# A hybrid decoder block on one core: gate corners in Y, another order in the b0 units, the second step's weights by quarters

## The chip, the core and the metric

The kernel runs on one core of a Trainium2 chip. The metric is the device time of one execution in microseconds, the median of several runs. A core has TensorE (PE) for matmuls, VectorE (DVE), ScalarE (ACT), GpSimd (POOL) and SyncE (SP). Each works through its own instructions in order. Here SP issues the weight loads, and POOL issues the transfers of gates, operands and rows.

## The reference, cut to what matters

```python
h = rmsnorm(x, norm_w)                                   # 256 tokens x 4096
u_p, z_p, u_c, b_c, c_c, z_c, g = split(h @ w_in)        # 6 x 2048 and 2 x 4096 columns
y_pool = pool(u_p, pool_w, pool_scale) * silu(z_p)
y_conv = b_c * conv3(c_c * u_c) * silu(z_c)
br0, br1 = y_pool @ w_branch[0], y_conv @ w_branch[1]    # 2048 -> 4096 each
merged = sigmoid(g0 + gate_b0) * br0 + sigmoid(g1 + gate_b1) * br1
out = rmsnorm(x + merged @ w_out, final_norm_w)
```

All is float32, and the weights (474 MB) are read once.

## The kernel before

**Units and steps.** The work is a list of units, each giving 1024 output columns for the 256 tokens: four conv units for each of two halves (cz, cb, cu, cc), pool units (pz, pu), eight gate units g0_0, g1_0, g0_1, ... g1_3, eight branch units b0_0, b1_0, b0_1, ... b1_3, and four output units o0 to o3. A unit has 16 steps (8 in a branch unit), each of which takes 256 input channels and 1 MB of weights. To keep precision, every operand is split into a rounded part and a remainder, and each product is three matmuls. A P step is the plain product of 2 x 2 blocks, 24 matmuls. An S step replaces the 8 block products by 7 (a Strassen-like scheme with sums of blocks), 21 matmuls. A string for each unit gives the order, such as `EIGHT = "PSPSPSPSPSPSPSPS"`; `B0 = "PPPPPSPS"` is that of the four b0 units and `B1 = "PSPSPSPP"` that of the b1 units.

**Weights.** A load on SP brings a step's weights into one of three raw buffers (`NRAW`, `issue_load`, L884). ACT rounds them into cells of a ring of 15 (`highs`, L205), DVE writes the remainders (`lows`, L209). For an S step DVE first adds up four sums into the tile `parts`, and ACT and DVE split these too. A load is issued when the step three places earlier in the list `loaded` has been prepared. Preparation runs some steps ahead of PE (`pump`, L899), as far as ring cells are free; the order in which instructions are written there is the order in which each engine runs them.

**Ends of units.** PE accumulates in four banks `sums` (E in the code) and, for S steps, four banks `shared` (F). When a bank of `sums` closes, ACT evacuates it to the tile E. The `shared` banks are copied by ACT to a place for four corners, `join.slot`, and DVE makes three sums there (`corner_sums`, L379). `combine` (L389) adds them to E. For most units the slot is a raw buffer: a Join stands in the list of loads and takes its turn (L868). For branch units (`rotates = False`) it is the tile `last_pair`, called `spare()`. If the last step is an S step, its matmuls are reordered so that `sums` closes first (`closing`, L346).

**Epilogues.** After a unit a queue of small jobs runs, one for each tick, that is for every six matmuls; `gap(n)` is n empty ticks. A gate unit (L617) has two accumulating transfers add the bias to E (`gather`, POOL), later two sigmoids on ACT and a store. A b0 unit multiplies its gate, loaded to Y, by E one tick after its end (`gap(1)`, L635). A b1 unit multiplies by the second gate, adds Y and transposes on PE. In the last gate unit and the branch units the operands of later units are filled in as well: POOL loads to stages sa and sb, ACT and DVE split them into `arena` (`pop_fill`, L726).

**The opening.** The first unit's operands are made from x as its steps go: `fetch_x(j)` loads step j's piece to Y, ACT scales and rounds it, DVE makes the remainder. In the code x's first piece is issued first (L961), then step 1's weights in four quarters, so that each can be rounded as it lands; step 2's piece and weights follow, these in one load. For step 3 and some later ones DVE also makes sums of operand blocks, with a copy in the tile `extra`.

Of the kernel before, what the change touches and what calls it, by code (L numbers as in the profile page):

```python
# [17 lines left out]
D = 4096  # L18
HALF = D // 2
NU = 1024  # L20
# [18 lines left out]
EIGHT = "PSPSPSPSPSPSPSPS"  # L39
HOST = "PPPBPPMMPPSPSSPSSPS"  # L40
OUT3 = "PSPSPSPSPSPSSPPP"
B0 = "PPPPPSPS"
B1 = "PSPSPSPP"


# [1 line left out]
def hybrid_block(ctx: ExitStack, tc: tile.TileContext, x, xc, prm, rows_in, w_in, pool_w, w_branch, w_out, out):  # L47
# [5 lines left out]
    def act(dst, src, func=AF.Copy, **kw):  # L53
        return pin(nc.scalar.activation(dst, src, func, **kw))  # L54

    def tt(dst, a, b, op):
        return pin(nc.vector.tensor_tensor(out=dst, in0=a, in1=b, op=op))  # L57

    def mul(dst, a, b):
        return tt(dst, a, b, ALU.mult)  # L60

    def add(dst, a, b):
        return tt(dst, a, b, ALU.add)
# [7 lines left out]
    def load(dst, src):  # L71
        return pin(nc.sync.dma_start(dst, src))
# [4 lines left out]
    def gather(dst, src):  # L77
        return pin(nc.gpsimd.dma_start(dst, src, accum_op=ALU.add))  # L78
# [6 lines left out]
    def sb(name, shape, dt=F32):  # L85
        return const.tile(shape, dt, name=name)
# [4 lines left out]
    E = sb("E", [P, 2, NU])  # L91
    Y = sb("Y", [P, 2, NU])
# [42 lines left out]
    last_pair = {}  # L135
# [69 lines left out]
    def highs(cells, src):  # L205
        for i, c in runs(cells):
            act(ring[:, c, 0], src[:, i])

    def lows(cells, src):  # L209
        for i, c in runs(cells):  # L210
            sub(ring[:, c, 1], src[:, i], ring[:, c, 0].bitcast(F32))
# [7 lines left out]
    def quarters(tile_):  # L219
        return tile_.rearrange("p a (b c) -> p (a b) c", c=NH)  # L220

    class Step:
# [7 lines left out]
        def first(self):  # L230
            if self.kind == "B":
                return []

            def rounded(cells):
                self.q = self.raw.rearrange("p (i c) -> p i c", i=4)
                self.cells = cells
                if self is steps[0]:
                    for i in range(4):
                        highs(cells[i:i + 1], self.q[:, i:i + 1])
                else:  # L240
                    highs(cells, self.q[:, 0:len(cells)])

            return [(3 if self.kind == "S" else 4, None, rounded)]

        def rest(self):
            if self.kind == "P":
                def rests(_):
                    if self is steps[0]:
                        for i in range(4):
                            lows(self.cells[i:i + 1], self.q[:, i:i + 1])  # L250
                    else:
                        lows(self.cells, self.q)

                return [(None, None, rests)] + self.mid
            if self.kind == "S":
                def added(_):
                    q = self.q
                    add(sums[:, 0:2], q[:, 3:4].to_broadcast([P, 2, NH]), q[:, 1:3])
                    add(sums[:, 2], sums[:, 0], q[:, 2])
                    add(sums[:, 3], sums[:, 2], q[:, 0])  # L260
                    lows(self.cells, q[:, 0:3])

                def split(cells):
                    self.sum_cells = cells
                    highs(cells[0:2], sums[:, 0:2])
                    highs(cells[2:4], sums[:, 2:4])
                    lows(cells, sums)

                return [(None, None, added)] + self.mid + [(4, None, split)]
            if self.kind == "B":  # L270
                def parts(cells):
                    self.cells = cells
                    highs(cells, quarters(E))
                    lows(cells, quarters(E))

                return [(4, lambda: self.unit.flags.get("base"), parts)]

            def pooled(cells):
                self.pool_cells = cells
                q = quarters(E)[:, 2 * self.g:2 * self.g + 2]  # L280
                highs(cells, q)
                lows(cells, q)

            return [(None, None, lambda _: lows(self.cells, self.q)),
                    (2, lambda: self.unit.flags.get(f"pooled{self.g}"), pooled)]
# [155 lines left out]
    def gap(n):  # L441
        return [None] * n
# [23 lines left out]
    def seq_x(text):  # L466
        if text is FIRST:
            return [("P", i) for i in FIRST]
        return sequence(text, ND, ND + NS + NB, NB)
# [4 lines left out]
    def in_unit(name, col, epi, text, **kw):  # L474
        units.append(Unit(name, lambda i: w_in[col // NU, i], seq_x(text), x_ops, epi, scaled=True, **kw))
        units[-1].text = text
        return units[-1]
# [139 lines left out]
    def gate_unit(n, c):  # L617
        def epi(u):
            def bias(t):
                gather(E[:, t], gate_b[n, None, c * NU:(c + 1) * NU].to_broadcast([P, NU]))  # L620

            return gap(1) + [lambda: bias(0), lambda: bias(1)] + gap(12) + [
                lambda: act(E[:, 0], E[:, 0], AF.Sigmoid), None,
                lambda: act(E[:, 1], E[:, 1], AF.Sigmoid), lambda: move(gates_d[n, c], E)] + (
                    [lambda: move(Y, gates_d[0, 0])] if (n, c) == (1, 3) else [])
        text = HOST if (n, c) == (0, 0) else SIX4 if (n, c) == (1, 3) else EIGHT
        in_unit(f"g{n}_{c}", 6 * HALF + n * D + c * NU, epi, text)

    def spare():
        return last_pair["tile"].rearrange("p (a n) -> p a n", a=2)  # L630

    def branch_unit(n, c):
        def epi(u):
            if n == 0:
                return gap(1) + [lambda: mul(Y, E, Y)]  # L635
            turned = spare() if c < 3 else Y

            def gated():
                mul(E, E, spare())
                if c == 3:  # L640
                    last_pair["stack"].close()
                    open_last(F32R)
                    last_pair["again"] = True

            def copy(j):
                act(chan(turned)[:, 2 * j:2 * j + 2], bankview(j))

            def stored():
                put(m_d[c], chan(turned))
                merged[c] = now[0] + STORED  # L650
            return [lambda: move(spare(), gates_d[1, c])] + gap(6) + [gated, lambda: add(E, E, Y), None,
                lambda: c < 3 and move(Y, gates_d[0, c + 1])] + gap(3) + pairs(transposes(E, copy)) + [stored]

        text = B1 if n else B0
        u = Unit(f"b{n}_{c}", lambda i: w_branch[n, c, i], seq_y(text), y_ops[n], epi)
        u.urgent, u.lead, u.rotates = (lambda: None), 3, False
        units.append(u)
# [106 lines left out]
    steps = [s for u in units for s in u.steps]  # L764
# [43 lines left out]
    def fetch_x(j):  # L808
        load(xt[:, j % 4].rearrange("p o c -> p (o c)"), xc[first_order[j]])
# [74 lines left out]
    def issue_load(s):  # L884
        i = s.load_index
        r = raw[:, i % NRAW]
        if isinstance(s, Join):
            s.slot = r.rearrange("p (i c) -> p i c", i=4)
            return
        if i == 0:  # L890
            for k in range(4):
                load(r[:, k * NH:(k + 1) * NH], s.src[:, k * NH:(k + 1) * NH])
        else:
            load(r, s.src)
        if i + 1 < 16:
            fetch_x(i + 1)
        s.raw = r
# [60 lines left out]
            state["limit"] = state["now"] + u.lead  # L958
        pump()

    fetch_x(0)  # L961
    pump()

    def room(o):
# [36 lines left out]
    for u in units:  # L1001
        if u.name == "b0_0":
            last_pair["stack"].close()
            open_last(F32)
        if not u.rotates:
            u.join.slot = last_pair["tile"].rearrange("p (i c) -> p i c", i=4)
        if u is last_x:
            bands_open.close()
            more = ctx.enter_context(tc.tile_pool(name="more", bufs=1))
            stages.append(more.tile([P, 8, P], F32, name="sb"))  # L1010
            queue_fills()
        if u is last:
            break
        for st in u.steps:
            assert st.prepared, (u.name, st.kind)
            run_step(u, st)
            state["now"] += 1
            if state["now"] == OPENED:
                opening.close()
                sums = ctx.enter_context(tc.tile_pool(name="parts", bufs=1)).tile([P, 4, NH], F32, name="parts")  # L1020
            pump()
            if u.before and st is u.steps[len(u.steps) * 3 // 4]:
                flush()
                u.before()
        flush()
        combine(u)
        queue.extend(u.epi(u))
        pump()
# [102 lines left out]
```

## Time and profile before

| | us |
|---|---|
| median of three runs | 2419.91 (2418.51 to 2421.69) |
| the profiled execution | 2420.03 |
| its span, first to last instruction | 2418.3 |
| PE busy | 2379.8 |
| DVE busy | 2137.6 |
| ACT busy | 1421.8 |

The span is divided as follows. The first unit's matmuls begin at 5.95 us, g1_3 ends and b0_0 begins at about 1708 to 1716 us, and the last matmul ends at 2406.9. PE's busy time is no measure of speed by itself, since matmuls overlap, but its idle time is time in which no matmul ran. In rows of the timeline the numbers are start and length in us; square brackets give the engine's idle time before the row and what ended it. L57 and L54 are helpers that record nearly all DVE and ACT work, so the tile names tell the operations apart.

### The profile page before, as it was taken

The page shows a single profiled execution, that of the slowest core. Times are in us where ns is not written, and L with a number is a line of the kernel's source. Part 1 is how long each engine was busy: PE and PEld are TensorE (multiplying, and loading weights), DVE is VectorE, ACT ScalarE, POOL GpSimd, SP SyncE. Part 2 cuts the span into 40 slices and gives each one's busy share as a digit, 9 for nine tenths or more (in the row PEclk, how much of TensorE's full clock was granted, in tenths as well). Part 3 has the DMA queues.
Part 4 walks back from the last instruction along what each step waited for, and adds up shares of the span by engine and source line. Part 5 has one row for each costly group of instructions (what it writes and reads, how often), then busy time and mean ns, then how long its engine had stood idle before and what let it go on. Part 6 is the DMA issues. An engine that isn't in the chain of part 4 may idle for free. (4 is left out here: it accounts for less than half of the span.)

```text
span 2418.3 us, 26848 instructions
## 1 busy us (share of the span) xinstructions
PE 2379.8 (98%) x10515; PEld 1960.6 (81%) x10515; DVE 2137.6 (88%) x1769; ACT 1421.8 (59%) x1367; POOL 85.6 (4%) x147
## 2 busy tenths in 40 slices
PE   8999999999999999999999999999899999999998
PEld 6888888888888888888888888888778887888886
DVE  8789989988989969969998999889788889899998
ACT  6655555655556556556666566665565555556664
POOL 0000000000000000000000000001100000000000
PEclk9999999999999999999999999999999999999999
DMA  8656546655646655655776576667666765758767
GB/s 331 225 193 226 191 175 244 234 199 204 220 177 231 228 192 192 225 191 187 266 244 204 215 261 242 209 224 272 229 245 212 264 233 208 257 192 273 246 217 267
DMA packets 82959, 547.07 MB, mean 226 GB/s; under 512 B 9488, under 2 KB 9488, under 8 KB 21776
## 3 DMA queue, kind: packets, MB, share of 16 engines
q1 hardware_dynamic: 69392, 485.52, 55.1%
q0 software_dynamic: 13008, 58.73, 8.0%
q8 instruction: 82, 1.34, 0.2%
q10 hardware_dynamic: 432, 1.11, 0.1%
q14 instruction: 45, 0.37, 0.0%
HBM read 519.10 MB, written 26.21 MB: 225 GB/s over the span
## 5 line engine op out<-in xcount | busy, mean ns | idle before, releaser
L937 PE MATMUL sums<-ring,arena 128*128 128x512 f32 x7515 | 1756.9, 391 | 20.5 <-DVE ring L57 9.4
L937 PEld LDWEIGHTS sums<-ring,arena 128*128 128x128 f32 x7515 | 1412.2, 188 | 319.7 <-DVE ring L57 12.3
L57 DVE TENSOR_TENSOR ring<-raw,ring 128x2048 fp32r<-128x2048 f32 (+3 forms) x526 | 938.6, 1796 | 167.0 <-ACT ring L54 163.5
L54 ACT ACTIVATE ring<-raw 128x2048 fp32r<-128x2048 f32 (+3 forms) x526 | 791.4, 1520 | 493.9 <-PE sums L937 270.9
L54 ACT ACTIVATE ring<-parts 128x1024 fp32r<-128x1024 f32 (+1 forms) x403 | 400.2, 1007 | 384.2 <-DVE parts L57 341.6
L937 PE MATMUL shared<-ring,arena 128*128 128x512 f32 x2100 | 509.2, 391 | 1.5 <-DVE ring L57 1.5
L57 DVE TENSOR_TENSOR ring<-parts,ring 128x2048 fp32r<-128x2048 f32 (+3 forms) x225 | 434.9, 1946 | 44.5 <-ACT ring L54 43.6
L937 PEld LDWEIGHTS shared<-ring,arena 128*128 128x128 f32 x2100 | 396.3, 189 | 86.3 <-DVE ring L57 3.6
L57 DVE TENSOR_TENSOR parts<-parts,raw 128x512 f32<-128x512 f32 x378 | 262.0, 693 | 12.9
L57 DVE TENSOR_TENSOR parts<-raw 128x1024 f32<-128x1024 f32 x189 | 230.8, 1221 | 7.5 <-DMA raw<-in_w_in_dram 7.2
L937 PE MATMUL sums<-ring,last_pair 128*128 128x512 f32 x366 | 89.8, 396 | 0.0
L937 PEld LDWEIGHTS sums<-ring,last_pair 128*128 128x128 f32 x366 | 68.9, 188 | 16.5
L57 DVE TENSOR_TENSOR raw<-raw 128x512 f32<-128x512 f32 (+1 forms) x66 | 57.3, 868 | 10.9 <-ACT raw L54 9.3
L54 ACT ACTIVATE E<-sums,rin 128x512 f32<-128x512 f32 x56 | 36.0, 687 | 25.5 <-PE sums L937 25.4
L54 ACT ACTIVATE raw<-shared 128x512 f32<-128x512 f32 x88 | 47.0, 606 | 0.3
L937 PE MATMUL shared<-ring,last_pair 128*128 128x512 f32 x168 | 41.6, 396 | 0.0
L937 PEld LDWEIGHTS shared<-ring,last_pair 128*128 128x128 f32 x168 | 31.6, 188 | 7.7
L69 DVE SCALAR_TENSOR_TENSOR E<-raw,rin,E 128x1024 f32<-128x1024 f32 x28 | 34.7, 1280 | 0.2
L54 ACT ACTIVATE last_pair<-shared 128x512 f32<-128x512 f32 x44 | 24.2, 600 | 13.8 <-PE shared L422 13.1
L57 DVE TENSOR_TENSOR E<-E,last_pair 128x2048 f32<-128x2048 f32 x12 | 27.4, 2287 | 2.2 <-ACT E L54 2.2
L78 POOL DMA_DIRECT2D E<-in_rows_dram x16 | 13.9, 867 | 434.4 <-DVE E L69 432.3
L54 ACT ACTIVATE E<-sums 128x512 f32<-128x512 f32 x44 | 25.6, 596 | 2.9 <-PE sums L937 0.5
(118 smaller groups left out, 553.9 us busy)
## 6 DMA issues: line engine op xcount, KB each, us to landing
raw<-in_w_in_dram SPq DMA_DIRECT2D x319, 1024.0 KB, 4.8
raw<-in_w_branch_dram SPq DMA_DIRECT2D x64, 1024.0 KB, 4.8
raw<-in_w_out_dram SPq DMA_DIRECT2D x64, 1024.0 KB, 4.8
E<-in_rows_dram POOLq DMA_DIRECT2D x16, 512.0 KB, 11.2
gates_d<-E POOLq DMA_DIRECT2D x8, 1024.0 KB, 8.2
Y<-in_xc_dram SPq DMA_DIRECT2D x16, 256.0 KB, 6.4
raw<-in_pool_w_dram SPq DMA_DIRECT2D x4, 1024.0 KB, 7.2
Y<-gates_d POOLq DMA_DIRECT2D x4, 1024.0 KB, 6.1
```

The source lines that it names most:

```text
L54: return pin(nc.scalar.activation(dst, src, func, **kw))
L57: return pin(nc.vector.tensor_tensor(out=dst, in0=a, in1=b, op=op))
L69: return pin(nc.vector.scalar_tensor_tensor(out=dst, in0=a, scalar=s, in1=b, op0=op0, op1=op1, **kw))
L78: return pin(nc.gpsimd.dma_start(dst, src, accum_op=ALU.add))
L937: pin(nc.tensor.matmul(ps, lhs, rhs, start=n == 0, stop=n == u.total[b] - 1))
```

## The change

There are three parts.

- Every gate unit gets `rotates = False`, and its corners go to Y instead of a raw buffer. Its Join so leaves the list of loads.
- The b0 order is PPPPSPSP instead of PPPPPSPS, and the product `Y = E * Y` comes after eight empty ticks instead of one.
- Step 2's weights are loaded, rounded and subtracted by quarters like step 1's. The first piece of x is issued after step 1's first quarter, no longer ahead of it.

```diff
-B0 = "PPPPPSPS"
+B0 = "PPPPSPSP"
...
-                if self is steps[0]:
+                if self in steps[:2]:
                     for i in range(4):
                         highs(cells[i:i + 1], self.q[:, i:i + 1])
...
-                    if self is steps[0]:
+                    if self in steps[:2]:
                         for i in range(4):
                             lows(self.cells[i:i + 1], self.q[:, i:i + 1])
...
-        in_unit(f"g{n}_{c}", 6 * HALF + n * D + c * NU, epi, text)
+        in_unit(f"g{n}_{c}", 6 * HALF + n * D + c * NU, epi, text).rotates = False
...
             if n == 0:
-                return gap(1) + [lambda: mul(Y, E, Y)]
+                return gap(8) + [lambda: mul(Y, E, Y)]
...
-        if i == 0:
+        if i < 2:
             for k in range(4):
                 load(r[:, k * NH:(k + 1) * NH], s.src[:, k * NH:(k + 1) * NH])
+                if i == k == 0:
+                    fetch_x(0)
         else:
             load(r, s.src)
...
-    fetch_x(0)
     pump()
...
         if not u.rotates:
-            u.join.slot = last_pair["tile"].rearrange("p (i c) -> p i c", i=4)
+            u.join.slot = quarters(Y if u.name[0] == "g" else spare())
```

## The prediction

> **What bounds the kernel now.** I read the page first (engines), then busy time and clock by stretches, then the timeline at the places where TensorE (PE) is not busy.
>
> ```profile
> span 2418.3 us, 26848 instructions
> ...
> PE 2379.8 (98%) x10515; PEld 1960.6 (81%) x10515; DVE 2137.6 (88%) x1769; ACT 1421.8 (59%) x1367; POOL 85.6 (4%) x147
> ```
> The span is 2418.3 us; the profiled run took 2420.03, so 1.7 us lie around it. The median of the three runs is 2419.91, 0.12 below. I subtract from 2420.03; the difference changes nothing. PE is busy 98% of the span and the change leaves its matmul count alone, so only its idle and its slow time can be won.
>
> ```profile
> 0.00:50.00 50.00, 42.61 (x168) 33.69 (x168) 39.09 (x63) 31.07 (x41) 1.53 (x7) 0.93 0.88 330
> ...
> 1700.00:1750.00 50.00, 42.86 (x182) 34.91 (x181) 37.65 (x40) 22.88 (x24) 5.54 (x9) 0.93 0.65 216
> 1750.00:1800.00 50.00, 46.85 (x197) 37.64 (x196) 46.36 (x35) 31.52 (x31) 0.00 (x0) 0.97 0.67 240
> ...
> 1712.20:1719.00 6.80, 3.42 (x8) 2.74 (x9) 3.91 (x7) 4.67 (x6) 0.00 (x0) 0.50 0.42 166
> ```
> The columns are the stretch, its length, busy time of PE, its weight loads, DVE, ACT and POOL, granted clock, DMA share and GB/s. The first three hold 7.4, 7.1 and 3.2 us of idle PE. The last shows a second loss: after a gap the granted clock is 0.50, here for 6.8 us.
>
> ```profile
> 1719.80 26.23 PE L937 MATMUL sums<-ring,arena 128*128 128x512 f32 x115
> ```
> This is the warm rate (timeline: start, length, engine, work, count): 26.23 / 115 = 0.228 us a matmul. A P step (24) takes 5.45 us, an S step (21) 4.77.
>
> **Part 1, the opening.** ACT rounds each weight tile as it lands, DVE then makes its remainder.
>
> ```profile
> 5.27 0.63 ACT L54 ACTIVATE ring<-raw 128x512 fp32r<-128x512 f32 x1 [0.39 <-DMA raw<-in_w_in_dram]
> ...
> 5.95 7.16 PE L937 MATMUL sums<-ring,arena 128*128 128x512 f32 x24 [0.84 <-ACT ring L54]
> 6.35 0.63 ACT L54 ACTIVATE ring<-raw 128x512 fp32r<-128x512 f32 x1 [0.46 <-DMA raw<-in_w_in_dram]
> ...
> 10.60 0.91 ACT L54 ACTIVATE arena<-Y,par 128x256 fp32r<-128x256 f32 x2 [0.17 <-DMA Y<-in_xc_dram]
> ...
> 13.08 1.91 ACT L54 ACTIVATE ring<-raw 128x2048 fp32r<-128x2048 f32 x1 [1.57 <-DMA raw<-in_w_in_dram]
> ...
> 15.02 2.29 DVE L57 TENSOR_TENSOR ring<-raw,ring 128x2048 fp32r<-128x2048 f32 x1 [2.99 <-ACT ring L54]
> ...
> 15.04 0.50 PE L937 MATMUL sums<-ring,arena 128*128 128x512 f32 x1 [1.94 <-ACT ring L54]
> 16.26 1.91 ACT L54 ACTIVATE ring<-raw 128x2048 fp32r<-128x2048 f32 x1 [0.47 <-DMA raw<-in_w_in_dram]
> ...
> 17.37 11.35 PE L937 MATMUL sums<-ring,arena 128*128 128x512 f32 x38 [1.82 <-DVE ring L57]
> ...
> 28.56 0.86 PE L937 MATMUL sums<-ring,extra 128*128 128x512 f32 x3
> ```
> ```profile
> 3.80:7.20 3.40, 2.56 (x10) 1.67 (x8) 1.76 (x4) 2.21 (x5) 0.00 (x0) 1.00 0.84 242
> ...
> 11.50:13.00 1.50, 1.50 (x8) 0.99 (x6) 0.53 (x2) 0.01 (x1) 0.00 (x0) 1.00 1.00 423
> ```
> Step 1 ends at 5.95 + 7.16 = 13.11. Step 2 has its rounded weights at 14.99, does one matmul, and has its remainders at 17.31: two gaps, 1.94 and 1.82. Then 38 matmuls take 11.35 us where 38 x 0.228 is 8.7: 2.7 lost to the half clock. The "extra" operand first serves the 16th matmul of step 3, so that step's second one ran 14 x 0.228 before 28.56, at 25.4.
>
> First quarter ahead of x: x is now second in SP's queue and should land where the first quarter does now, at 5.2. ACT then rounds x (0.91) and the quarter (0.63), and PE starts at 6.8 instead of 5.95. I price it 0: step 1's end hangs on its last quarter, which does not move, and step 3 decides in any case (below). Without that cover it costs 0.9.
>
> Step 2 by quarters: three more issues on SP, which is ahead here; nothing. ACT pays 4 x 0.63 for 1.91. Its first quarter can be rounded at 11.5, behind x's 0.91, and step 2 runs from about 13.3 to 18.8 without a gap. What is late next is step 3. In the last two rows the 2 KB rows of step 1's quarters move at 242 GB/s at a share of 0.84 (288 at full share), whole rows at 423. So 1.05 MB by quarters takes 3.6 us, not 2.5, and step 3's weights behind it land at 17.4, not 16.26. With rounding 1.91 and remainder 2.29 step 3's second matmul comes at 21.7 instead of 25.4: 3.7 won. Bounds: 20.9 if quarters are no slower (DVE's operand sums then decide), 22.3 if they come 1.08 apart like the first two of step 1 (6.35 - 5.27). The new gap is 18.8 to 21.7 less one matmul, 2.4 to 2.7 us. A half clock after it costs 1.6 (row at 1780.48, part 3) to 2.7 (row at 17.37). A gap of 2.80 us brought it there; I charge 1.0. **Net 2.7**, from 0.4 to 4.5.
>
> The Trainium skill ("TensorE: Matmul & The Clock Gate", Why this matters for your kernels) allows idle gaps up to about 3 us before the clock falls back; by that the net would be 3.7, but the 2.80 us gap did not agree. The Trainium skill ("DMA: Bandwidth & Descriptors", Specifications) has line rate from 512 B up; by that the quarters would cost nothing and the restart come at 20.9. The two rows of stretches disagree.
>
> **Part 2, corners in Y.** Before, a gate unit's corner sums hold one of the three raw buffers until the unit is combined.
>
> ```profile
> 1699.03 2.29 DVE L57 TENSOR_TENSOR ring<-raw,ring 128x2048 fp32r<-128x2048 f32 x1
> ...
> 1702.66 5.78 PE L937 MATMUL sums<-ring,last_pair 128*128 128x512 f32 x24
> ...
> 1713.05 1.91 ACT L54 ACTIVATE ring<-raw 128x2048 fp32r<-128x2048 f32 x1 [6.91 <-DMA raw<-in_w_branch_dram]
> 1714.86 2.41 ACT L54 ACTIVATE E<-sums,rin 128x512 f32<-128x512 f32 x4
> ...
> 1715.59 4.61 PE L937 MATMUL sums<-ring,arena 128*128 128x512 f32 x12 [7.14 <-ACT E L54]
> ```
> ```profile
> raw<-in_w_branch_dram SPq DMA_DIRECT2D x64, 1024.0 KB, 4.8
> ```
> At g1_3's end ACT has the rounding of b0_0's third step queued ahead of the four evacuations. It waits 6.91 us for those weights, so the evacuations start at 1714.86 and PE stands for 7.14. Then twelve matmuls take 4.61 (warm 12 x 0.228 + 0.2 = 2.9): 7.14 + about 1.9 = 9.0 lost. With Y the third load needs only the buffer of g1_3's last step, free at 1699.03 + 2.29 = 1701.3, and 4.8 us (the page's median to landing) later, at 1706.1, it is there. Rounding ends at 1708.1, the first evacuation (2.41 / 4) at 1708.7; PE ends g1_3 at 1708.4, so about 0.5 remains: **gain 8.5**. A landing of 6.6 us makes it 6.7. The corners are as many instructions as before; Y's previous reader is work of an earlier unit or of g0_0's middle. I find no such gap in the seven other gate units and count nothing there.
>
> **Part 3, the b0 units.** PPPPSPSP puts both S steps one earlier and ends with P. The product Y = E*Y comes seven ticks (42 matmuls, 9.6 us) later.
>
> ```profile
> 1759.96 7.39 PE L937 MATMUL sums<-ring,arena 128*128 128x512 f32 x30 [0.33 <-ACT E L54]
> ...
> 1765.51 2.67 DVE L57 TENSOR_TENSOR last_pair<-last_pair 128x512 f32<-128x512 f32 x3
> ...
> 1772.62 2.29 DVE L57 TENSOR_TENSOR Y<-E,Y 128x2048 f32<-128x2048 f32 x1
> ...
> 1779.08 2.29 DVE L57 TENSOR_TENSOR ring<-parts,ring 128x2048 fp32r<-128x2048 f32 x1
> 1779.22 1.44 PE L937 MATMUL sums<-ring,arena 128*128 128x512 f32 x5 [2.80 <-DVE ring L57]
> 1780.48 4.50 PE L937 MATMUL shared<-ring,arena 128*128 128x512 f32 x12
> ...
> 1867.18 1.43 PE L937 MATMUL sums<-ring,arena 128*128 128x512 f32 x5 [0.58 <-DVE ring L57]
> ...
> 1953.72 1.43 PE L937 MATMUL sums<-ring,arena 128*128 128x512 f32 x5 [0.58 <-DVE ring L57]
> ...
> 2000.21 1.09 PE L422 MATMUL shared<-ident,E 128*128 128x128 f32 x8 [0.68 <-DVE E L57]
> ...
> 2044.22 2.50 PE L937 MATMUL sums<-ring,arena 128*128 128x512 f32 x5 [3.65 <-DVE ring L57]
> ```
> In all four DVE runs corner sums (2.67), combine (the product's shape, 2.3) and product ahead of an S step's remainder, and PE waits 2.80, 0.58, 0.58 and 3.65. With the half clock (4.50 for twelve that need 2.9; at b0_3 five in 2.50 for 1.3 besides) and the small waits at 1759.96 the four cost about 5.2, 0.8, 0.8 and 6.4. In the changed order DVE prepares a P and an S step of b1 before the combine, and the product stands behind a further S and P step.
>
> From 1772.62 to 1779.08 lie the product, 2.2 to the next start as for any 2048 columns, and an S step's additions and remainder, 4.3. b0_1, b0_2: once PE has ended P6 (b0's sixth step) and ACT has rounded b1's first step in its ring cells (1.9), DVE has P 2.2, S 4.3, corner sums 2.7, the S step's sums 2.2, P 2.2, combine 2.3, S 4.3 = 20.2 us to the remainder of b1's second S step. PE gets there after S, P, P, S, P = 25.9. Lead 25.9 - 1.9 - 20.2 = 3.8, no wait: **gain 1.6**. The transposes' 0.68 at 2000.21 wait for E + Y, which now finds its S step done earlier: **gain 0.8** with its start.
>
> b0_3: the chain carried on to b1_3's third S step takes 37.9 (20.2, then sums 2.2, P 2.2, product 2.3, S 4.3, and 6.7 of operand fills) against 36.1 of PE. The first rounding here comes in two pieces and hides. So PE waits 1.8 there and 0.6 at the sums: 2.4 instead of 6.4, **gain 4.0** (0 to 6.4).
>
> b0_0 comes right behind g1_3 now, and there a wait takes the old one's place:
>
> ```profile
> 1717.20 1.02 DVE L57 TENSOR_TENSOR sb<-sb 128x128 f32<-128x128 f32 x4
> ...
> 1719.92 2.47 DVE L69 SCALAR_TENSOR_TENSOR E<-raw,rin,E 128x1024 f32<-128x1024 f32 x2
> ...
> 1722.69 0.86 POOL L78 DMA_DIRECT2D E<-in_rows_dram  x1 [0.32 <-DVE E L69]
> 1725.50 0.57 POOL L75 DMA_DIRECT2D sa<-y_d  x1 [1.94 <-DVE arena L57]
> ...
> 1738.43 0.63 ACT L54 ACTIVATE arena<-sa 128x512 fp32r<-128x512 f32 x1 [0.17 <-DMA sa<-y_d]
> ```
> An operand fill on DVE takes 2.7 (1717.20 to 1719.92), the combine 2.47. POOL issues two bias gathers (the second at 1722.69) and then sa's fill, which ACT has 12.9 us later. DVE's order from 1701.3 (fill 2.7, P 2.2, 0.6, P 2.2, sums 2.7, P 2.2, fill 2.7, combine 2.4) puts the gathers at 1719 and this fill at 1722; behind the gathers, under fewer weight loads, I let it land at 1733. ACT has it ahead of P6's rounding: 0.6 + 1.9 + 2.2 gives 1737.3, where PE (1708.9 + 26.6) is at 1735.5. Stall 1.8, between 0 and 7.6 (landing no earlier than now). At the end the S step's sums are ahead of the evacuations on ACT: 0.6. 5.2 - 2.4, **gain 2.8** (-3.0 to 5.2).
>
> Sum: 2.7 + 8.5 + 1.6 + 0.8 + 4.0 + 2.8 = 20.4; 2420.03 - 20.4 = **2399.6**.
>
> **Rivals.** (a) DVE bounds the b stage: it is busy 46.36 of the 50 us from 1750, so the waits of b0_0 and b0_3 come back at the next S steps. Against it speaks the lead of 3.8 in b0_1. 4.0 + 2.8 less: 2406.4. (b) The opening gives nothing, because quarters trail and the clock halves (22.3, 1.6, 0.9 at the start): 2402.3, at worst 2404. (c) The fill lands in time and DVE's lead holds in b0_3: 1.8 + 2.4 more, 2395.4. (e) Quarters move like whole rows, at 423 GB/s, so step 3 restarts at 20.9 and the gap, under 2 us, stays between the 0.58 that left the clock full and the 2.80 that did not: 0.8 + 1.0 more, 2397.8. This is what the two pages of the Trainium skill named above would make of the opening. (d) Slower: the b0 units now end with P, so at each change to b1 ACT has a rounding and an S step's sums ahead of the evacuations, the pattern of 1713.05. If that waits for weights each time, 9.0 comes four times: 2435.6. It decides from 20.4 / 4 = 5.1 us a change. Against it: the S step's raw buffer is free some 10 us ahead, and b1's ends have the pattern without such a gap.
>
> **How the numbers follow.** Forecast 49% (its own range 2395 to 2404), (a) 17%, (b) 12%, (c) 8%, (e) 8%, (d) 6%. The range 2391 to 2409 takes in (b), (a) with 1.6 and a half clock besides, and (c) with (e) and the last 2.6 of part 3's and part 2's small waits. A measurement of this kernel can tell about 0.2% (4.8 us) from no change: faster 0.91, within 0.03 (the tail of (a)), slower 0.06.
>
> **What would show it.** Right: no gap between 13 and 17 us and one of 2 to 3 at about 19; at g1_3's end PE idle under 1 us at clock 1.00; no wait over 0.6 in b0_1 and b0_2; a stall at b0_0's P6 that ACT's fill of sa ends; one of about 2 in b1_3. Wrong: ACT waiting for w_branch ahead of evacuations, or DVE without idle time and waits of 3 us in b1_0 and b1_3.

## The result, and the profile after

The changed kernel takes 2396.78 us (median of 4 runs, 2395.70 to 2397.47), the kernel before 2419.42 (4 runs, 2418.51 to 2421.69): a ratio of 0.9905, 95% interval 0.9887 to 0.9922, or 22.6 us less. The profiled run took 2395.70, 24.3 less than the profiled run of before. Its page:

```profile
span 2394.0 us, 26867 instructions
...
PE 2372.0 (99%) x10515; PEld 1956.6 (82%) x10515; DVE 2136.9 (89%) x1770; ACT 1421.8 (59%) x1368; POOL 85.7 (4%) x147
...
L939 PE MATMUL sums<-ring,arena 128*128 128x512 f32 x7515 | 1751.5, 390 | 6.3 <-DVE ring L57 2.9
```

```profile
L937 PE MATMUL sums<-ring,arena 128*128 128x512 f32 x7515 | 1756.9, 391 | 20.5 <-DVE ring L57 9.4
```

DVE and ACT are busy as long as before. PE does the same matmuls in 7.8 us less of busy time, because less of it passes at a slow clock, and its idle time is 16.5 us less: ahead of its largest group 6.3 us of idle time are left, where before (the last row) had 20.5. What PE waited for (us in total, times, longest), before and then after:

```profile
PE sums L937 <- DVE ring L57: 9.4, 5, 3.7
PE sums L937 <- ACT E L54: 7.5, 2, 7.1
...
PE shared L422 <- DVE E L57: 2.1, 3, 1.2
```
```profile
PE sums L939 <- DVE ring L57: 2.9, 1, 2.9
...
PE shared L422 <- DVE E L57: 0.2, 1, 0.2
```

Of five waits for DVE's remainders (four ahead of S steps, one in the opening) one is left, the 7.5 for evacuations into E are gone from the list, and the transposes wait 0.2 where they waited 2.1. The same by stretches (first from:to, then the length and the busy times; the last three numbers are the granted clock, the DMA share and GB/s), after, and one row of before:

```profile
4.60:7.40 2.80, 1.04 (x4) 0.53 (x3) 1.43 (x3) 2.01 (x5) 0.00 (x0) 1.00 1.00 373
...
17.40:22.60 5.20, 5.20 (x24) 4.04 (x23) 5.20 (x6) 4.37 (x7) 0.00 (x0) 1.00 0.89 337
...
1700.00:1750.00 50.00, 49.74 (x218) 40.44 (x217) 46.94 (x44) 31.20 (x32) 5.00 (x8) 1.00 0.84 282
1750.00:1800.00 50.00, 50.00 (x222) 41.43 (x221) 47.05 (x31) 28.74 (x26) 0.53 (x1) 1.00 0.70 253
...
2016.00:2028.00 12.00, 12.00 (x54) 9.67 (x53) 11.90 (x12) 4.76 (x4) 0.54 (x1) 1.00 0.57 194
2030.60:2037.40 6.80, 6.06 (x14) 4.79 (x15) 6.80 (x5) 4.43 (x5) 0.54 (x1) 0.50 0.58 202
```
```profile
2043.40:2050.10 6.70, 5.88 (x14) 4.64 (x15) 6.63 (x8) 3.94 (x4) 0.00 (x0) 0.50 0.53 166
```

The stretches from 1700 and 1750 have 0.3 us of idle PE in 100, where before had 10.3. One half clock is left, 6.8 us from 2030.6, and before had the same at that place. The timeline:

```profile
6.87 16.20 PE L939 MATMUL sums<-ring,arena 128*128 128x512 f32 x63 [1.76 <-ACT ring L54]
...
22.91 0.86 PE L939 MATMUL sums<-ring,extra 128*128 128x512 f32 x3
...
1696.98 5.78 PE L939 MATMUL sums<-ring,last_pair 128*128 128x512 f32 x24
...
1700.35 1.92 ACT L54 ACTIVATE ring<-raw 128x2048 fp32r<-128x2048 f32 x1 [1.44 <-DMA raw<-in_w_branch_dram]
...
1702.17 2.40 ACT L54 ACTIVATE E<-sums,rin 128x512 f32<-128x512 f32 x4
...
1702.90 23.45 PE L939 MATMUL sums<-ring,arena 128*128 128x512 f32 x102
...
1714.91 0.57 POOL L75 DMA_DIRECT2D sa<-y_d  x1 [1.94 <-DVE arena L57]
...
1724.64 0.63 ACT L54 ACTIVATE arena<-sa 128x512 fp32r<-128x512 f32 x1 [6.28 <-DMA sa<-y_d]
...
1740.13 1.49 ACT L54 ACTIVATE ring<-raw 128x1536 fp32r<-128x1536 f32 x1 [1.95 <-DMA raw<-in_w_branch_dram]
...
1977.77 1.03 PE L422 MATMUL shared<-ident,E 128*128 128x128 f32 x8
...
2029.53 1.75 DVE L57 TENSOR_TENSOR ring<-raw,ring 128x1536 fp32r<-128x1536 f32 x1
...
2031.34 2.50 PE L939 MATMUL sums<-ring,arena 128*128 128x512 f32 x5 [2.93 <-DVE ring L57]
...
2033.64 4.68 PE L939 MATMUL shared<-ring,arena 128*128 128x512 f32 x12
```

Set beside the rows of before, these starts tell where the time was won. The first "extra" matmul of step 3 ran at 28.56 and runs at 22.91: 5.65 us from the opening. The first matmul of b0_0 ran at 1715.59 and runs at 1702.90, 12.69 earlier: 7.0 more. The transposes of 2000.21 start at 1977.77, 22.44 earlier: another 9.75 from the half clock behind g1_3's end and from b0_0, b0_1 and b0_2. The end of the span is 24.3 earlier: only 1.9 from there on.

### The profile page after: what moved, and what is told of

It is laid out like the page before. It is cut to its first block, busy times and chain, and to the rows that moved or that the text cites. A ratio compares the mean times of both kernels' runs of the same rounds, so it can differ in the third digit from the quotient of the medians.

```text
span 2394.0 us, 26867 instructions
## 1 busy us (share of the span) xinstructions
PE 2372.0 (99%) x10515; PEld 1956.6 (82%) x10515; DVE 2136.9 (89%) x1770; ACT 1421.8 (59%) x1368; POOL 85.7 (4%) x147
## 3 DMA queue, kind: packets, MB, share of 16 engines
q8 instruction: 82, 1.34, 0.2%
## 5 line engine op out<-in xcount | busy, mean ns | idle before, releaser
L57 DVE TENSOR_TENSOR ring<-raw,ring 128x1536 fp32r<-128x1536 f32 (+3 forms) x528 | 938.6, 1789 | 142.8 <-ACT ring L54 139.0
L54 ACT ACTIVATE ring<-raw 128x1536 fp32r<-128x1536 f32 (+3 forms) x528 | 790.7, 1515 | 460.3 <-PE sums L939 286.5
L939 PEld LDWEIGHTS sums<-ring,last_pair 128*128 128x128 f32 x366 | 68.9, 188 | 16.5
L57 DVE TENSOR_TENSOR raw<-raw 128x512 f32<-128x512 f32 (+1 forms) x42 | 36.5, 869 | 10.3 <-ACT raw L54 9.3
L54 ACT ACTIVATE raw<-shared 128x512 f32<-128x512 f32 x56 | 29.7, 610 | 0.4 <-DVE ring L57 0.2
L54 ACT ACTIVATE Y<-shared 128x512 f32<-128x512 f32 x44 | 23.8, 598 | 4.8 <-PE shared L422 4.7
```

Source lines behind the costliest of these rows:

```text
L939: pin(nc.tensor.matmul(ps, lhs, rhs, start=n == 0, stop=n == u.total[b] - 1))
```

## The experiments

Each of the change's three parts was run alone, and each was left out; two runs took one edit of the opening each; four vary the changed kernel. "Opening" is the hunk on the first loads with the rounding by quarters, "corners" the two lines with rotates and Y, "order" the string B0 with the gap of 8.

| Kernel | us, median (runs) | before, same chip | ratio, 95% interval |
|---|---|---|---|
| 1 opening alone | 2416.65 (11) | 2419.28 | 0.9989, 0.9980 to 0.9998 |
| 2 quarters alone | 2417.01 (11) | 2419.28 | 0.9988, 0.9979 to 0.9997 |
| 3 x second alone | 2417.16 (11) | 2419.28 | 0.9992, 0.9983 to 1.0000 |
| 4 corners alone | 2409.29 (5) | 2419.28 | 0.9961, 0.9949 to 0.9974 |
| 5 order alone | 2409.75 (5) | 2419.75 | 0.9957, 0.9945 to 0.9970 |
| 6 changed less opening | 2402.98 (5) | 2419.75 | 0.9928, 0.9916 to 0.9941 |
| 7 changed, product early | 2396.50 (4) | 2419.75 | 0.9906, 0.9893 to 0.9920 |
| 8 changed, product late in b0_3 | 2395.52 (4) | 2419.75 | 0.9900, 0.9885 to 0.9915 |
| 9 changed less corners | 2403.19 (5) | 2417.37 | 0.9941, 0.9928 to 0.9953 |
| 10 changed less order | 2407.37 (5) | 2417.37 | 0.9957, 0.9945 to 0.9970 |
| 11 as 8, x first | 2394.65 (4) | 2417.37 | 0.9904, 0.9888 to 0.9919 |
| 12 as 11, fills held | 2397.86 (4) | 2417.37 | 0.9916, 0.9902 to 0.9930 |

**1. The opening alone** (before, with these lines and the rounding by quarters of the change):

```diff
-        if i == 0:
+        if i < 2:
             for k in range(4):
                 load(r[:, k * NH:(k + 1) * NH], s.src[:, k * NH:(k + 1) * NH])
+                if i == k == 0:
+                    fetch_x(0)
...
-    fetch_x(0)
     pump()
```

> The kernel before with the opening's two edits only (first quarter of step 1's weights ahead of x; step 2's weights by quarters). In the changed kernel the first 'extra' matmul of step 3 ran at 22.91 us against 28.56 before, so theory A (the opening is worth twice what was predicted) expects 5.7 us: 2413.7. The prediction's own term was 2.7: 2416.7. Rival: the earlier landings of the changed kernel are run-to-run luck of the DMA queue, then the last quarter of step 1 lands near 9.8 us again and the time is 2416 to 2419.

The opening itself does what it does in the changed kernel: the "extra" matmul starts at 23.86, 4.7 us earlier. But the whole kernel gains 2.6 (0.5 to 4.8 by the interval): near the prediction's 2.7, and for another reason. Rows of its timeline, and of before at the same place of the program:

```profile
23.86 0.86 PE L939 MATMUL sums<-ring,extra 128*128 128x512 f32 x3
...
1662.33 0.63 ACT L54 ACTIVATE arena<-sa 128x512 fp32r<-128x512 f32 x1 [3.61 <-DMA sa<-y_d]
...
1674.72 1.43 PE L939 MATMUL sums<-ring,arena 128*128 128x512 f32 x5 [1.14 <-DVE ring L57]
...
1688.91 2.11 PE L939 MATMUL shared<-ring,arena 128*128 128x512 f32 x8 [1.49 <-DVE ring L57]
```
```profile
1663.25 0.63 ACT L54 ACTIVATE arena<-sa 128x512 fp32r<-128x512 f32 x1 [0.93 <-DMA sa<-y_d]
...
1689.84 2.11 PE L937 MATMUL shared<-ring,arena 128*128 128x512 f32 x8 [0.31 <-DVE ring L57]
```

ACT has an operand fill (arena from sa) ahead of the rounding of a P step, and waits 3.61 us for sa's transfer, where it waited 0.93: the transfer is issued 3.6 us earlier than before (at 1651.99, not 1655.59) and is there only 0.9 earlier. So PE waits 1.14 and 1.49 for the remainders behind it; before had the second alone, at 0.31. Of the 4.7 us that the opening won, 0.9 are left where g1_3's last step begins (1701.76, before 1702.66). Most of the loss falls in g1_3, 1650 us after the opening.

**2 and 3. One edit of the opening at a time.** Run 2 is run 1 with x first again; run 3 is run 1 with step 2's load and rounding whole:

```diff
 (2)
-                if i == k == 0:
-                    fetch_x(0)
...
+    fetch_x(0)
     pump()
 (3)
-        if i < 2:
+        if i == 0:
```

> The kernel before with step 2's weights by quarters only; x stays first in the queue. Theory A1: what held step 1's last quarter back (landed 9.77 us) was the whole load behind it, with rows four times as long, which took most of the bandwidth; with quarters behind it, it lands at 7.3 to 7.6, PE starts at 5.95 as before, step 3's weights land at about 15.2, a gap of up to 1.1 us opens ahead of step 3, and the gain is 5.5 to 6: 2413.4 to 2413.9. Theory A2: the place of x did it; then the last quarter stays near 9.8, step 3's weights come at about 17.4 and the time is 2416 to 2418.

> The kernel before with x behind the first quarter only; step 2's weights are one whole load. Theory A1: the last quarter still lands at 9.5 to 10, PE starts about 0.9 us later (6.8), the two gaps at 13 and 15 us stay, and the time is 2419 to 2420.5 (no gain). Theory A2: the last quarter lands at about 7.4, everything behind it 2 us earlier, and the time is 2416.5 to 2418.

PE's rows in run 2, in run 3 and, with the opening untouched, in run 4 (its last two rows are for the next paragraph):

```profile
5.63 17.34 PE L937 MATMUL sums<-ring,arena 128*128 128x512 f32 x63 [0.52 <-ACT ring L54]
22.80 0.86 PE L937 MATMUL sums<-ring,extra 128*128 128x512 f32 x3
```
```profile
7.21 8.66 PE L939 MATMUL sums<-ring,arena 128*128 128x512 f32 x25 [2.10 <-ACT ring L54]
16.10 8.94 PE L939 MATMUL sums<-ring,arena 128*128 128x512 f32 x38 [0.22 <-DVE ring L57]
24.87 0.86 PE L939 MATMUL sums<-ring,extra 128*128 128x512 f32 x3
```
```profile
5.66 7.28 PE L937 MATMUL sums<-ring,arena 128*128 128x512 f32 x24 [0.54 <-ACT ring L54]
14.21 0.49 PE L937 MATMUL sums<-ring,arena 128*128 128x512 f32 x1 [1.28 <-ACT ring L54]
16.54 11.76 PE L937 MATMUL sums<-ring,arena 128*128 128x512 f32 x38 [1.83 <-DVE ring L57]
...
1709.99 28.88 PE L937 MATMUL sums<-ring,arena 128*128 128x512 f32 x126 [1.58 <-ACT E L54]
...
1770.33 1.43 PE L937 MATMUL sums<-ring,arena 128*128 128x512 f32 x5 [1.99 <-DVE ring L57]
```

Either edit alone takes most of the gain. In run 4 PE waits 1.28 and 1.83 and then does 38 matmuls in 11.76 us, at half clock for a while; in run 3 it starts at 7.21 instead of 5.66, finds step 2 all but ready (0.22) and does the same 38 in 8.94. Starting later, without a gap afterwards, saved the clock: 2.8 us (the first 25 matmuls of run 3 take 8.66 us, though, the first 24 of run 4 7.28). In run 2 there is no gap either, from an early start on. Neither theory on the queue holds as put. Step 1's last quarter takes from issue to landing 7.1 us in before, 6.3 in run 4, 5.9 in run 3, 5.8 in run 2, 4.9 in run 1 and 4.8 in the changed kernel: the untouched opening alone differs by 0.8. All traces of this case together part more clearly: 6.3 to 7.1 us with the opening untouched (four), 5.8 to 6.2 with quarters alone (runs 2, 11, 12), 5.9 with x second alone, and 4.7 to 5.3 with both (six). PE's progress does not follow that order. The "extra" matmul starts at 27.57 to 28.59, at 22.80 to 23.27, at 24.87, and at 22.91 to 24.51. So the quarters alone do for PE what both edits do, and nothing shows that putting x second adds to them. By whole times the three can't be told apart.

**4. Corners alone.**

```diff
-        in_unit(f"g{n}_{c}", 6 * HALF + n * D + c * NU, epi, text)
+        in_unit(f"g{n}_{c}", 6 * HALF + n * D + c * NU, epi, text).rotates = False
...
-            u.join.slot = last_pair["tile"].rearrange("p (i c) -> p i c", i=4)
+            u.join.slot = quarters(Y if u.name[0] == "g" else spare())
```

> The kernel before with the gate units' corners in Y only. Theory A: the 9.0 us at g1_3's end go but for 0.4 (as the changed kernel shows) and the old b0_0 behind it keeps its 5.2: 2410.8. Rival: the old order of b0_0 can't use the earlier start, its fills and gathers come no earlier, and its stall grows by part of what was won: 2413 to 2416.

10.0 us (6.3 to 12.3 by the interval), in the median more than theory A's 8.6 although 1.58 are left at g1_3's end (the row at 1709.99): b0_0's wait, the row at 1770.33, fell from 2.80 to 1.99, and the twelve matmuls behind it take 3.05 us instead of 4.50. The rival is out: b0_0 did not lose by the earlier start, it gained.

**5. Order alone.**

```diff
-B0 = "PPPPPSPS"
+B0 = "PPPPSPSP"
...
-                return gap(1) + [lambda: mul(Y, E, Y)]
+                return gap(8) + [lambda: mul(Y, E, Y)]
```

> The kernel before with the b0 units' order and the later product only. Theory A: b0_1 and b0_2 give 1.9, the transposes 1.0, b0_3 0.6 (as in the changed kernel's trace), and b0_0 2.8, the part of its 5.1 that the corners alone did not give: 6.3, 2413.0. The prediction's own terms give 1.6 + 0.8 + 4.0 + 2.8 = 9.2: 2410.1. Rival: b0_0 needs the earlier start, and without it nothing is won there: 2415.8.

```profile
1713.39 26.19 PE L937 MATMUL sums<-ring,arena 128*128 128x512 f32 x102 [5.67 <-ACT E L54]
```

Also 10.0 (7.3 to 13.3): theory A and the rival are out. The prediction's own 9.2 fits as a sum, though two of its terms do not (see below). g1_3's end still costs PE 5.67, but in b1_0 there is no wait of PE left. So corners and order each remove b0_0's stall, wholly or in part, and their gains overlap there.

**6. The changed kernel without the opening** (the hunks of run 1 taken out).

> The changed kernel without the opening's two edits (corners, order and product kept). Theory A: behind a kernel that no longer waits for loads and operand fills near the gate units' end, the opening keeps all of what it wins in its own stretch (5.7 by the two profiles), so this is 2402.4. Rival: it is worth what the opening alone gave (2.6): 2399.4.

2402.98, nearer theory A: beside the other two parts the opening is worth 6.2 by the medians and 5.6 by the ratios, alone 2.6. With 2 to 4 us to either side of each ratio, the times alone don't part the two for certain; the traces do (runs 9 and 10).

**7. Product early.**

```diff
-                return gap(8) + [lambda: mul(Y, E, Y)]
+                return gap(1) + [lambda: mul(Y, E, Y)]
```

> The changed kernel with the product back right behind the combine (one tick). By the prediction's chain the order alone leaves DVE 1.5 us of lead in b0_1 and b0_2 with the product in front (3.8 less 2.3), and in b0_3 the product comes ahead of the second S step instead of the third, so a wait of about 2.3 comes there and one of 0.7 at the third. Theory A (the order carries the gain, the product's place is worth little): 2395 to 2398. Rival (the product's place carries it): waits of 2 us or more come back in b0_0 and b0_3 with the half clock behind them, 2400 to 2404.

```profile
2020.91 1.42 PE L939 MATMUL sums<-ring,arena 128*128 128x512 f32 x5 [1.91 <-DVE ring L57]
...
2032.29 1.43 PE L939 MATMUL sums<-ring,arena 128*128 128x512 f32 x5 [0.70 <-DVE ring L57]
```
```profile
2020.50:2023.50 3.00, 2.59 (x11) 1.96 (x12) 3.00 (x3) 3.00 (x3) 0.00 (x0) 1.00 0.49 139
```

2396.50, theory A: the product's place is worth nothing in sum, and the order carries part 3. The transposes of b1_3 wait 2.30 for their sum here, where those of the changed kernel waited at most 0.2. In b0_3 the wait of 2.93 becomes two, 1.91 and 0.70, and the granted clock (last row) stays 1.00 behind the first.

**8. Product late in b0_3 alone.**

```diff
-                return gap(8) + [lambda: mul(Y, E, Y)]
+                return gap(8 if c < 3 else 14) + [lambda: mul(Y, E, Y)]
```

> The changed kernel with the product of b0_3 alone six ticks later still, behind b1_3's third S step on DVE; PE, ACT and the queues keep their orders. Theory A: the 2.9 us wait of b1_3 is DVE's chain, so it shrinks by the product's 2.3 to about 0.6, the half clock behind it (3.1) goes with it, and the time is 2391.5. Rival: DVE has no slack anywhere in b1_3, the wait comes back in the next P step or at the corner sums: 2394.5 to 2397.

```profile
2029.93 1.43 PE L939 MATMUL sums<-ring,arena 128*128 128x512 f32 x5 [0.72 <-DVE ring L57]
...
2032.73 2.14 PE L939 MATMUL shared<-ring,arena 128*128 128x512 f32 x8 [0.47 <-DVE ring L57]
...
2037.13 9.14 PE L939 MATMUL sums<-ring,arena 128*128 128x512 f32 x39 [1.34 <-DVE ring L57]
```
```profile
PE shared L422 <- DVE E L57: 1.7, 2, 1.5
```

The half clock goes and the wait at the third S step shrinks to 0.72, as theory A has it; but 0.47 and 1.34 appear behind the product's new place, and the transposes wait 1.7 for their sum (last row, from the list of waits) where they waited 0.2. 1.3 us less than the changed kernel in the medians, within what the measurement can tell: nearer the rival.

**9 and 10. The changed kernel without corners, and without order.** What keeps the opening's gain?

> The kernel before with the opening and the b0 units' order and product, corners left in the raw buffers. Alone the opening gave 2.6, beside corners and order 6.2. Theory O (the order, which also moves the operand fills ahead of b0_0, is what keeps the opening's gain from being lost near the gate units' end): 2409.8 less about 5.5, 2404.2. Theory C (the corners keep it): 2409.8 less 2.6, 2407.2.

> The kernel before with the opening and the corners in Y, b0 units as before. Theory C (the corners free the raw buffer that the opening's gain is lost on): 2409.3 less about 5.5, 2403.8. Theory O (it is the order): 2409.3 less 2.6, 2406.7.

```profile
1662.10 0.63 ACT L54 ACTIVATE arena<-sb 128x512 fp32r<-128x512 f32 x1 [2.64 <-DMA sb<-y_d]
...
1685.10 2.14 PE L939 MATMUL shared<-ring,arena 128*128 128x512 f32 x8 [0.35 <-DVE ring L57]
```
```profile
1661.51 0.63 ACT L54 ACTIVATE arena<-sa 128x512 fp32r<-128x512 f32 x1 [2.98 <-DMA sa<-y_d]
...
1688.09 2.14 PE L939 MATMUL shared<-ring,arena 128*128 128x512 f32 x8 [1.28 <-DVE ring L57]
```

Run 9 gains 14.2, 4.2 more than the order alone, and run 10 gains 10.0, as much as the corners alone. That points to theory O, but does not decide by itself: each ratio is known to about 3 us, and the kernel before ran 2.4 us faster on this chip than on the one that the expected times start from. The traces decide. From the first "extra" matmul to the start of g1_3's last step PE takes 1674.10 us before. With the new order it takes 1673.3 to 1674.7 in all eight traces; with the old order and the opening untouched 1674.50 (run 4); with the old order and a changed opening 1677.90, 1678.43, 1675.74 and 1676.45 (runs 1, 2, 3 and 10). So the gain is lost only with the old order, in run 10 with corners in Y as well: theory O. The order of the b0 units also sets the order in which their operands are filled, in the gate units ahead of them. With the old order ACT waits 2.98 for sa ahead of the P step's rounding, and PE 1.28; with the new one it waits for sb (2.64) at another place, and PE 0.35. That the fills are the link is read from these rows; moving them alone was not tried.

**11. As 8, with x first again** (the edit of run 2).

> The changed kernel with b0_3's product behind b1_3's third S step (as in the run before this) and x first in SP's queue again; step 2's weights stay in quarters. Theory A1 (the quarters behind step 1 carry the opening; x behind the first quarter only delays PE's start by 0.9 to 1.2): step 3's first extra operand at 22.8 instead of 23.7, 2394.0 to 2395.0. Rival (the place of x matters): the first quarters trail again, 2396 to 2398.

The "extra" matmul starts at 23.27, between the two theories; 2394.65 by the median, but a ratio of 0.9904 where the changed kernel has 0.9905. No version here is shown to beat the changed kernel.

**12. As 11, with the operand fills of b1_3 held back.**

```diff
+    hold = set()
...
-                return gap(8 if c < 3 else 14) + [lambda: mul(Y, E, Y)]
+                if c == 3:
+                    def product():
+                        mul(Y, E, Y)
+                        hold.clear()
+                    return gap(8) + [lambda: hold.add(1)] + gap(5) + [product]
+                return gap(8) + [lambda: mul(Y, E, Y)]
...
+            if hold and force is None:
+                break
             if f.at is not None and f.free() and (now[0] >= f.at + LANDING or f.o is force):
```

> The kernel of the run before it (product late, x first) with the operand fills of b1_3's first half held back until that product. Theory A (DVE's chain ahead of b1_3's third S step is what is too long, by the fills as much as by the product): the waits of 0.72, 0.47 and 1.34 go, 2.0 to 2.5 less than the run before: 2391.5 to 2393. Rival (the fills are late then for o0, whose wait of 1.5 grows by what was saved, or DVE has no room for them later): 2394 to 2397.

```profile
2046.85 1.91 ACT L54 ACTIVATE ring<-raw 128x2048 fp32r<-128x2048 f32 x1 [4.52 <-DVE sb L57]
...
2048.67 2.04 ACT L54 ACTIVATE E<-sums 128x512 f32<-128x512 f32 x4
...
2049.30 2.93 PE L945 MATMUL sums<-ring,arena 128*128 128x512 f32 x6 [3.71 <-ACT E L54]
```

The third S step runs without a wait and a P step waits 0.74; but the held fills come when b1_3 ends, a rounding on ACT waits 4.52, by the profile for a held fill's sums on DVE, with the evacuations behind it, and PE waits 3.71. The rival, by more than it said: DVE's work in b1_3 can be moved, not hidden.

## Why the prediction was right, and where it was not

The forecast of 20.4 us less came out as 22.6, with its signs right; three sizes were wrong, two too small and one too large. In the two profiles they are off by 3.0, 2.4 and -3.3 us: that the sum came within 2.2 us is in part luck.

- **Part 1, 2.7 forecast, 5.65 in the trace** (4.5 on the means of all traces: the "extra" matmul at 23.8 in six with the changed opening, at 28.2 in four with the old). Right: PE starts at 6.8 (6.87), no gap between 13 and 17. Wrong: "its last quarter, which does not move" and "step 3's weights behind it land at 17.4". The last quarter came 2.3 us sooner after its issue (7.1 to 4.8), and step 3's weights 8.5 after theirs, at 15.2 (issue at 6.72). The 288 GB/s that I took for rows of 2 KB was not a property of the rows: step 2's whole load, issued at 3.61, was under way in that stretch too, and in the changed kernel from 4.6 to 7.4 the quarters move at 373 GB/s at a share of 1.00. So there is no gap at 19: 63 matmuls run without one from 6.87, and the clock is 1.00 from 17.4 to 22.6, where it was half. The Trainium skill ("DMA: Bandwidth & Descriptors", Specifications), by which rows from 512 B up go at line rate, was nearer than the 288 that I worked out, though whole rows had 423; rival (e), which it stood beside, was right for the opening: its 4.5 is less than in this trace, but equals the mean of all. Why the queue moved less in that stretch before is open; part of it differs from run to run (7.1 and 6.3 us with one and the same opening).
- **That the opening's gain is kept** was a step I did not write down. Alone it is not: 4.7 us in its own stretch are 0.9 at g1_3's last step in the same trace, because a later wait (ACT's for an operand fill) is ended by a transfer and not by PE. The traces of all runs (see runs 9 and 10) show that the order of the b0 units keeps it.
- **Part 2, 8.5 forecast.** The wait of 7.14 is gone. The third load is there when ACT asks for it, but for 1.44; evacuations start at 1702.17, and 102 matmuls run from 1702.90 in 23.45, with no half clock. With the 4.61 for twelve that needed 2.9 that is 8.8, and 0.1 is left between 1696.98 + 5.78 and 1702.90. Left out of the changed kernel (run 9), corners are worth 0.9941 - 0.9905, 8.7 us too, give or take 5. In the other runs with corners in Y up to 1.88 us of this wait are left.
- **b0_1, b0_2 and the transposes, 1.6 + 0.8 forecast.** No such wait is left, and the transposes' total fell from 2.1 to 0.2, with one of 1.2 among it that I had not counted. The reason was half right: run 7 shows that turning the order did it and the product's place did not matter, as the lead of 3.8 that I worked out, larger than the product's 2.3, would have told me.
- **b0_0, 2.8 forecast, all of its 5.2 won.** The step that failed: "I let it land at 1733". sa's fill is issued 12.0 us behind b0_0's first matmul, not 13, and lands 9.7 us later, not 11. ACT does wait for it, 6.28 us, but from 1724.64 on rounding and remainder are just done when PE comes there; PE does not wait. The mechanism was there without its price: rival (c) in this unit.
- **b0_3, 4.0 forecast, about 0.7 won.** The mechanism was right, at the step named: DVE is busy 11.90 of 12 us from 2016, and the third S step's remainder ends at 2031.28. The wait is 2.93, not 1.8. "The first rounding here comes in two pieces and hides" was the error: ACT begins it at 1992.33, behind a wait of 3.24 that PE ends, and DVE its remainder at 1993.84. From there to 2031.28 are 37.4 us, the chain of 37.9; it began 2.0 after PE had ended P6, where I had let it begin at once. And I charged no half clock behind this stall, although a gap of 2.80 had brought one in my own rows: the 17 matmuls from 2031.34 end at 2038.32, 3.1 later than 17 x 0.228 would have them. The same followed before (0.50 from 2043.4 to 2050.1), so only the difference of the waits was won. Rival (a) was right here and wrong in b0_0.
- **Rival (d), the slower side.** ACT waits 1.95 us for weights at 1740.13, at the first change from b0 to b1, but PE's list has no wait for E's evacuations any more: the S step's buffer is free early enough, the reason that I gave.

The Trainium skill ("TensorE: Matmul & The Clock Gate", Why this matters for your kernels) allows gaps up to about 3 us. The gap of 2.93 halved the clock for 6.8 us, and gaps of 1.28 and 1.83 with one matmul between them lowered it too (run 4, 0.57 on the mean from 15 to 23 us). Length alone does not decide. A single gap of 1.88 left 0.63 over the next 3.4 us (run 10, at 1708.62), while 1.91 (run 7) and 1.99 (run 4, at 1770.33) left 1.00. A gap of 2.76 left 0.55 in run 2 (at 1776.60) and 1.00 in run 3 (at 1775.90). Every gap of 2.80 or more between matmuls in these traces lowered it. So 3 us is too many here.

## What to carry to other kernels

Every gap of PE that a forecast leaves standing is to be charged with the half clock if it is 2.8 us or more (every such gap lowered the clock here), and with a chance of it from 1.9 us up (1.88 and one of 2.76 did, 1.99 and another of 2.76 did not). Two gaps with a single matmul between them are best counted as one (0.79 and 1.82 in run 6 left 0.61). Such a stall can cost twice: 2.93 us of gap and 3.1 of slow clock. A gain early in a kernel is kept only if every later wait is ended by the engine that now comes earlier; look for those that a transfer ends, first of all operand fills queued ahead of weight rounding on one engine. Where two edits remove the same stall, their gains alone need not add up: that 2.6 + 10.0 + 10.0 is 22.6 here says little, since an overlap in b0_0 and a help of the one for the other are both in it.

## What the runs showed that was not expected

A later start of PE can be the cheaper one: 1.6 us later, with no gap afterwards, it saved 2.8 us of half clock (runs 3 and 4, one trace each). And one and the same first loads take up to 0.8 us more or less from run to run (6.3 to 7.1 us from issue to landing in the four traces with the opening of before), a part of what I had read as a rate of the rows.
